# A two-layer decoder trunk on one core: last down tile in two accumulators, down stages in plain order, deferred transposes moved

## The chip, the cores and the metric

One NeuronCore of one Trainium2 chip runs the whole kernel as one program. The metric is device time in microseconds, from the program's start to its end, taken as the median of several executions. Separately, one execution was recorded by the hardware profiler; its trace gives the start and the duration of each instruction on TensorE (PE; its weight loads are PEld), VectorE (DVE), ScalarE (ACT), GpSimd (POOL) and SyncE (SP).

## What is computed

The reference is a two-layer decoder trunk on 256 tokens of width 1024. Cut to what matters here:

```python
def swiglu(x, w_gate, w_up, w_down):
    return (jax.nn.silu(x @ w_gate) * (x @ w_up)) @ w_down

for layer in range(DEPTH):                       # 2 layers
    if layer == N_A_LAYERS:                      # before layer 1
        shared_kv = shared_moba_kv(h, positions, kv_norm_g, w_kv, k_norm_g)
    h = h + 0.5 * swiglu(rms_norm(h, ffn1_norm_g[layer]), ...)
    hn = rms_norm(h, mix_norm_g[layer])
    ...                                          # layer 0: convolution module; layer 1: causal attention
    mem_out = memory_attention(...)              # both layers
    h = h + jnp.concatenate([primary, mem_out], axis=-1) @ w_o[layer]
    h = h + 0.5 * swiglu(rms_norm(h, ffn2_norm_g[layer]), ...)
return h
```

There are four feed-forward blocks of this kind, with an inner width of 2816. All is in 32-bit floating point.

## The kernel before

The four feed-forward blocks are called a, b, c and d and are calls of one function, `ffn` (L353). Everything is kept transposed: features on the 128 partitions, the 256 tokens along the free dimension. A tile of the stream is 128 features, so the width is 8 tiles (`KD`) and the inner width 22 (`KF`).

Precision is bought by splitting. Each weight half-chunk of 128x1024 that the SP queue brings in as `raw` is split into a high part `wh` (a copy on ScalarE that rounds) and a low part `wl` (a subtraction on VectorE). The activations are kept as high and low halves side by side. One product of a 128x128 weight tile with a tile of activations is then high x high, high x low and low x high. There are two ways to issue it:

- `mm2` (L259), a *pair*: one matmul of 512 columns with the high weights over both halves of the activations, and one of 256 columns with the low weights. The result lies in two halves of a PSUM bank, which `both_halves` (L280) adds later: a copy of the second half on ScalarE and an addition on VectorE. `mm2_lo_first` (L271) is the same pair with the low matmul first.
- `mm3` (L252), a *triple*: three matmuls of 256 columns into one half of a bank. It needs no addition afterwards.

Each block has a gate stage and a down stage. In the gate stage, for each of the 22 inner tiles `j`, eight pairs make the gate product (tiles named `ag`, `bg`, `cg`, `dg`) and eight the up product (`au`, `bu`, `cu`, `du`); ScalarE and VectorE turn them into two halves of a hidden tile `hs[:, j]`. In the down stage (L453 to L483), for each of the 8 output tiles `m`, 22 products with the hidden tiles accumulate in one bank (`ao`, `bo`, `co`, `do`). For `m` from 0 to 6 these are pairs, and odd ones have the low matmul first, so the order on TensorE is high, low, low, high, high, low and so on. The last tile, `m` = 7, is 22 triples, so that its eviction is short: the next stage, or the end of the kernel, waits for it. VectorE scales the sum by 0.5 and the norm's factor (`scalar_tensor_tensor`) and adds it to the residual `x` (`tensor_tensor`). Block d then stores each tile.

Small steps are put between the pairs of the gate stage by a plan: a dictionary from (tile `j`, `"g"` or `"u"`, product `k`) to a step. `mean` makes the norm's mean squares (tiny matmuls, `anrp`, `bnrp`, `dnrp`), `rows` spreads the norm's factors over partitions with two transposes (`anbp`, `bnbp`, `cnbp`, `dnbp`). Other planned steps are *turns*: two transposes each that bring a group of keys from token order into head order (`to_heads_T`, L511; tiles `mk1p` for the memory keys of layer 1 in block b, `sk2p` for the last shared keys in block c). In `mm2` a planned step is placed between the pair's high and its low matmul: the transposes are ordered behind the high one, the low one behind the last transpose.

The tile framework schedules each engine's instructions and may change their order, unless the kernel says otherwise. `state["order"]` names engines whose instructions stay in the program's order ("P" is TensorE). Before the change it is "P" from the end of layer 0's output projection (L1139) through block b's first four inner tiles, and empty for the rest of b and for blocks c and d. Layer 1's mixing part between c and d has a list written out by hand (`MIX1`) with all engines in order. The weights flow through three buffers of `raw` and four each of `wh` and `wl`; the accumulators through four PSUM banks, with two more named "aux" for transposes and the like.

Of the kernel before, what the change touches and what calls it, by code (L numbers as in the profile page):

```python
# [9 lines left out]
F32 = mybir.dt.float32  # L10
# [4 lines left out]
ALU = mybir.AluOpType  # L15
AX = mybir.AxisListType

P = 128
# [6 lines left out]
HD = 64  # L25
# [50 lines left out]
e5.a e6.x lo18 e6.h hi19 e7.x e6.l e6.q e7.h lo19 e6.a e7.q e7.a e7.l  # L76
""".split()
AHEAD = 3

POOL_NORM = (1,)  # L80

# [28 lines left out]
def tile_kernel(ctx: ExitStack, tc: tile.TileContext, w, xT, memT, pos, vec, hg, const, spec, out):  # L110
# [39 lines left out]
    nc.vector.memset(mhalf, -0.5)  # L150


    state = {"chunk": 0, "half": 0, "raw": None, "order": "", "last": {}, "between": None, "made": []}

    class Ordered:

# [19 lines left out]
    def behind(i, other):  # L176
        tc.add_manual_dep(i.ins, other.ins.name,
                          mybir.DependencyInfo(mybir.DependencyClass.NoSync, mybir.DependencyReason.DATA),
                          reason="issue order")
# [13 lines left out]
    def mmul(*a, **k):  # L193
        return in_order("P", nc.tensor.matmul(*a, **k))  # L194
# [64 lines left out]
    def mm2(o, wt, y, k, first, last, turn=None):  # L259

        h, l = wt
        a = mmul(o, h, y[:, k].rearrange("p a s -> p (a s)"), start=first, stop=False)
        if turn is not None:
            state["between"] = a
            turn()
            last_turn, state["between"] = state["between"], None
        b = mmul(o[:, :SEQ], l, y[:, k, 0], start=False, stop=last)
        if turn is not None:
            behind(b, last_turn)

    def mm2_lo_first(o, wt, y, k, last):  # L271
        h, l = wt
        mmul(o[:, :SEQ], l, y[:, k, 0], start=False, stop=False)
        mmul(o, h, y[:, k].rearrange("p a s -> p (a s)"), start=False, stop=last)

    def mm_group2(o, y, turns):
        for k, wt in enumerate(tiles_of(1)):
# [51 lines left out]
    def rstd_cols(name, acc):  # L329
        v = mean_cols(name, acc)  # L330
        r = tp.tile([P, NT], F32, name=name, tag="rc", bufs=3)
        gps.tensor_tensor(r, v, mhalf[:, :NT], op=ALU.pow)
        return r
# [17 lines left out]
        return tp.tile([P, SEQ], F32, name=name, tag="acc")  # L351

    def ffn(name, y, acc, nexts, store=False, quick=False, hook=None, after=None, hook_down=None, r=None, plan=None,  # L353
            early=None, turns=()):


        plan = plan or {}
# [9 lines left out]

        def rows():
            norm["rb"] = bcast_rows(name + "nb", norm["r"])
            for turn in turns:  # L370
                turn()

        def planned(j, which):
            return {k: {"mean": mean, "rows": rows}.get(what, what) for (jj, w_, k), what in plan.items()
# [12 lines left out]
        for j in range(KF):  # L387
# [27 lines left out]
            else:  # L415
# [10 lines left out]
                else:  # L426
                    mm_group2(pg, y, planned(j, "g"))
                    mm_group2(pu, y, planned(j, "u"))
            if early and j == 3:
                state["order"] = ""  # L430
            if j == 0 and "mean" not in plan.values() and r is None:
                mean()
            if rb is None and j < rows_at[0]:
# [19 lines left out]
        for m in range(KD):  # L453
            po = psum(f"{name}o{m}")
            if hook_down:
                with tc.issue_after(state["act"].ins):
                    hook_down(m)

            both_sums = m < KD - 1
            for k in range(KF):  # L460
                if both_sums and k % 2:
                    mm2_lo_first(po, next(it), hs, k, k == KF - 1)
                elif both_sums:
                    mm2(po, next(it), hs, k, k == 0, False)
                else:
                    mm3(po[:, :SEQ], next(it), hs, k, k == 0, k == KF - 1)
            if both_sums:
                d = both_halves(f"{name}d{m}", po, "g")
                dve.scalar_tensor_tensor(d, d, 0.5, rb, op0=ALU.mult, op1=ALU.mult)
            else:  # L470
                d = tp.tile([P, SEQ], F32, name=f"{name}d{m}", tag="g")
                dve.scalar_tensor_tensor(d, po[:, :SEQ], 0.5, rb, op0=ALU.mult, op1=ALU.mult)
            dve.tensor_tensor(x[:, m], d, x[:, m], op=ALU.add)
            if store:
                nc.sync.dma_start(out[m], x[:, m])
                continue
            last = quick and m == KD - 1
            if last:
                square_sum(f"{name}q{m}", acc, x[:, m], False, dve)
            for yy, g in zip(ys, nexts):  # L480
                state["ends"] = scaled_split(yy, x[:, m], m, g, last)
            if not last:
                square_sum(f"{name}q{m}", acc, x[:, m], m == 0)  # L483
# [280 lines left out]
    def memory1(m):  # L764
        if not my1:
# [1 line left out]
        mem_prep(1, my1[0], (m,))  # L767

    (y,), acc = ffn("a", y, None, (V_MIX,), quick=True, hook=prepare, after=AF.Exp, hook_down=memory1,
                    plan={(2, "u", 1): "mean", (3, "g", 3): "rows"})  # L770

    hc = cp.tile([P, KF * 2 * SEQ], F32, name="hc", tag="hs")
    taken = [0]
# [368 lines left out]
    def sum_squares():  # L1142
# [7 lines left out]
        for t, tt in found:  # L1150
            key1.normed(t, tt)
        state["order"] = "P"

    (ykv, y), acc = ffn("b", y, acc, (V_KV, V_FFN1 + KD), plan={(2, "u", 1): "mean", (3, "g", 3): "rows"},
                        early=sum_squares, turns=mem_turns)


    rkv = rstd_cols("rkv", acc)
    turns = []
    kuse = [keys(f"sk{i}", rkv, G_K, kTs, 2 * i, True, turns if i == 2 else None, 1) for i in range(3)]  # L1160
# [2 lines left out]
    proj("kv1", ykv, kuse[2], vuse[0])  # L1163
    proj("kv2", ykv, vuse[1], vuse[2])
    (y,), acc = ffn("c", y, acc, (V_MIX + KD,), after=AF.Exp, r=rkv,
                    plan={(2, "g", 4): lambda: [turn() for turn in turns]})
    qT = cp.tile([P, KD, SEQ], F32, name="q1T", tag="t8k")
    cat = y_tiles("cat1")
    ys = y_tiles("oby")
# [307 lines left out]
        steps[name]()  # L1477
    state["order"] = ""
    y, acc = ys, sums
    ffn("d", y, acc, (), store=True, plan={(2, "g", 4): "rows"})  # L1480
    assert state["chunk"] * CH * P == w.shape[0] * CH * P, state


# [147 lines left out]
```

## Time and profile before

| what | value |
|---|---|
| median of 3 executions | 961.93 us (961.75 to 964.14) |
| the profiled execution | 963.06 us |
| its span in the trace | 961.3 us |
| TensorE busy | 953.0 us, 5670 matmuls and as many weight loads |
| VectorE, ScalarE, GpSimd busy | 721.9, 575.1, 90.0 us |

A row of a group tells the line, the engine, the operation, what is written and read (`bo<-bhs,wh`: tile `bo` from the hidden tiles and the high weights), the shape and the number, then durations. L194 and L197 are the helpers through which all matmuls and all transposes are issued, and L164 the one for VectorE, ScalarE and GpSimd, so one goes by the tiles' names. A matmul's recorded duration reaches into the next one, since they are pipelined: what a matmul costs is the distance from its start to the next one's start. A timeline row gives a start and a length in us.

### The profile page before, as it was taken

The page shows a single profiled execution, that of the slowest core. Times are in us where ns is not written, and L with a number is a line of the kernel's source. Part 1 is how long each engine was busy: PE and PEld are TensorE (multiplying, and loading weights), DVE is VectorE, ACT ScalarE, POOL GpSimd, SP SyncE. Part 2 cuts the span into 40 slices and gives each one's busy share as a digit, 9 for nine tenths or more (in the row PEclk, how much of TensorE's full clock was granted, in tenths as well). Part 3 has the DMA queues.
Part 4 walks back from the last instruction along what each step waited for, and adds up shares of the span by engine and source line. Part 5 has one row for each costly group of instructions (what it writes and reads, how often), then busy time and mean ns, then how long its engine had stood idle before and what let it go on. Part 6 is the DMA issues. An engine that isn't in the chain of part 4 may idle for free.

```text
span 961.3 us, 15012 instructions
## 1 busy us (share of the span) xinstructions
PE 953.0 (99%) x5670; PEld 832.1 (87%) x5670; DVE 721.9 (75%) x1263; ACT 575.1 (60%) x1057; POOL 90.0 (9%) x89
## 2 busy tenths in 40 slices
PE   8999999999999999999999999999999999999998
PEld 6888888897888888888988888888897998888887
DVE  6898777776889877767767777767779578777663
ACT  6676566556686655655556665555548666556442
POOL 0122000110012000000123000000134120000000
PEclk9999999999999999999999999999999999999999
DMA  8755455454346555555555555555552245555550
GB/s 293 289 200 188 176 194 200 176 176 152 111 137 222 187 200 175 193 201 176 185 196 189 176 184 208 179 181 205 183 177 74 103 175 182 207 181 182 208 203 21
DMA packets 26569, 174.11 MB, mean 181 GB/s; under 512 B 3329, under 2 KB 4865, under 8 KB 6145
## 3 DMA queue, kind: packets, MB, share of 16 engines
q1 hardware_dynamic: 26208, 172.99, 50.5%
q8 instruction: 44, 0.72, 0.3%
q10 hardware_dynamic: 288, 0.17, 0.1%
q14 instruction: 29, 0.23, 0.1%
HBM read 172.10 MB, written 1.05 MB: 180 GB/s over the span
## 4 chain that ended last, share of the span: by engine, by line
PE 93%; DVE 4%; DMA 1%; ACT 1%; issue 0%; POOL 0%; SPq 0%
PE cg L194 8%; PE do L194 6%; PE ao L194 6%; PE co L194 6%; PE bo L194 6%; PE bu L194 6%; PE dg L194 6%; PE cu L194 6%; PE du L194 6%; PE bg L194 6%; PE ag L194 6%; PE au L194 6%; PE kv L194 3%; PE obo L194 2%; PE mkv L194 2%; DVE room L164 2%
## 5 line engine op out<-in xcount | busy, mean ns | idle before, releaser
L164 DVE TENSOR_TENSOR wl<-raw,wh 128x1024 fp32r<-128x1024 f32 (+1 forms) x326 | 395.8, 1216 | 168.7 <-ACT wh L164 166.8
L164 ACT ACTIVATE wh<-raw 128x1024 fp32r<-128x1024 f32 (+1 forms) x326 | 341.1, 1050 | 296.1 <-PE dg L194 27.1
L194 PE MATMUL ag<-y,wh 128*128 128x512 f32 x176 | 63.7, 398 | 0.5 <-ACT wh L164 0.5
L194 PE MATMUL au<-y,wh 128*128 128x512 f32 x176 | 63.4, 396 | 0.0
L194 PE MATMUL bg<-oay,wh 128*128 128x512 f32 x176 | 62.4, 393 | 0.1
L194 PE MATMUL dg<-oby,wh 128*128 128x512 f32 x176 | 62.5, 392 | 0.0
L194 PE MATMUL cu<-by,wh 128*128 128x512 f32 x176 | 62.3, 393 | 0.0
L194 PE MATMUL du<-oby,wh 128*128 128x512 f32 x176 | 62.3, 391 | 0.0
L194 PE MATMUL cg<-by,wh 128*128 128x512 f32 x176 | 62.2, 392 | 0.0
L194 PE MATMUL bu<-oay,wh 128*128 128x512 f32 x176 | 62.2, 392 | 0.0
L194 PE MATMUL bo<-bhs,wh 128*128 128x512 f32 (+1 forms) x198 | 55.8, 368 | 0.0
L194 PE MATMUL co<-chs,wh 128*128 128x512 f32 (+1 forms) x198 | 55.8, 368 | 0.0
L194 PE MATMUL do<-dhs,wh 128*128 128x512 f32 (+1 forms) x198 | 55.8, 368 | 0.0
L194 PE MATMUL ao<-ahs,wh 128*128 128x512 f32 (+1 forms) x198 | 55.8, 368 | 0.0
L194 PE MATMUL ag<-y,wl 128*128 128x256 f32 x176 | 48.9, 280 | 2.2 <-DVE wl L164 2.2
L194 PE MATMUL cg<-by,wl 128*128 128x256 f32 x176 | 49.4, 281 | 0.0
L194 PE MATMUL bg<-oay,wl 128*128 128x256 f32 x176 | 49.4, 281 | 0.0
L194 PE MATMUL bu<-oay,wl 128*128 128x256 f32 x176 | 49.4, 281 | 0.0
L194 PE MATMUL dg<-oby,wl 128*128 128x256 f32 x176 | 49.4, 280 | 0.0
L194 PE MATMUL cu<-by,wl 128*128 128x256 f32 x176 | 49.3, 280 | 0.0
L194 PE MATMUL du<-oby,wl 128*128 128x256 f32 x176 | 49.3, 280 | 0.0
L194 PE MATMUL au<-y,wl 128*128 128x256 f32 x176 | 48.7, 279 | 0.0
(960 smaller groups left out, 2242.9 us busy)
## 6 DMA issues: line engine op xcount, KB each, us to landing
raw<-in_w SPq DMA_DIRECT2D x158, 1024.0 KB, 4.8
raw<-in_w SPq DMA_DIRECT2D x5, 512.0 KB, 10.4
mT<-in_memT SPq DMA_DIRECT2D x1, 1024.0 KB, 8.4
out<-x SPq DMA_DIRECT2D x8, 128.0 KB, 1.7
dft<-in_spec SPq DMA_DIRECT2D x1, 817.0 KB, 10.2
raw<-in_w SPq DMA_DIRECT2D x2, 256.0 KB, 3.9
x<-in_xT SPq DMA_DIRECT2D x1, 512.0 KB, 8.8
x<-in_xT SPq DMA_DIRECT2D x2, 128.0 KB, 3.2
```

What stands on the lines that cost most here:

```text
L164: i = f(*a, **k)
L194: return in_order("P", nc.tensor.matmul(*a, **k))
```

## The change

Four edits, all in how TensorE's instructions are issued.

1. A planned step is placed behind the pair's low matmul, and the next pair's high matmul is ordered behind it, where it was between the high and the low one.
2. The turns are planned one by one. In b, the two turns of the memory keys, which followed the rows' two transposes directly (six in one place), come one pair and two pairs later. In c, the two turns, planned together at inner tile 2, product 4, are at tile 2, product 6 and at tile 3, product 4.
3. In the down stages of b, c and d all pairs are in plain order (high, low); block a keeps the alternating order. TensorE's program order is kept from inner tile 3 on to the end of these blocks. In the first down tile, behind the third pair, something is computed that nothing reads: in b one bfloat16 matmul of 64 columns, in c two transposes of the identity, in d one product of 256 columns from the pair's own operands.
4. The last down tile of all four blocks is split over two banks: the first 14 products (`APART`) are pairs in one bank, which is evicted and added to `x` while the last 8, as triples, accumulate in another, which is then scaled and added to `x` as before.

```diff
+APART = 14
...
     def mm2(o, wt, y, k, first, last, turn=None):
         h, l = wt
         a = mmul(o, h, y[:, k].rearrange("p a s -> p (a s)"), start=first, stop=False)
-        if turn is not None:
-            state["between"] = a
-            turn()
-            last_turn, state["between"] = state["between"], None
+        if state["held"] is not None:
+            behind(a, state["held"])
+            state["held"] = None
         b = mmul(o[:, :SEQ], l, y[:, k, 0], start=False, stop=last)
         if turn is not None:
-            behind(b, last_turn)
+            state["between"] = b
+            turn()
+            state["held"], state["between"] = state["between"], None
...
+    def unread_little(wt, y):
+        mmul(psum("ul", "aux", 2)[:, :HD], busy[:, :P], busy[:, :HD], start=True, stop=True)
+
+    def unread_product(wt, y):
+        mmul(psum("ue", "aux", 2)[:, :SEQ], wt, y, start=True, stop=True)
+
+    def unread_turns(wt, y):
+        pu = psum("ut", "aux", 2)
+        for i in range(2):
+            transp(pu[:, i * P:(i + 1) * P], ident, ident)
...
-            if early and j == 3:
-                state["order"] = ""
+            if j == 2 and not first:
+                state["order"] = "P"
...
-            both_sums = m < KD - 1
-            for k in range(KF):
-                if both_sums and k % 2:
-                    mm2_lo_first(po, next(it), hs, k, k == KF - 1)
-                elif both_sums:
-                    mm2(po, next(it), hs, k, k == 0, False)
-                else:
-                    mm3(po[:, :SEQ], next(it), hs, k, k == 0, k == KF - 1)
...
+            whole = KF if m < KD - 1 else APART
+            for k in range(whole):
+                if lo_first and k % 2:
+                    mm2_lo_first(po, next(it), hs, k, k == whole - 1)
                 else:
+                    wt = next(it)
+                    mm2(po, wt, hs, k, k == 0, k == whole - 1 and not lo_first,
+                        (lambda: settle(wt[0], hs[:, k, 0])) if settle and (m, k) == (0, 2) else None)
+            d = both_halves(f"{name}d{m}", po, "g")
+            into_x(d, d)
+            if m == KD - 1:
+                po = psum(f"{name}o{m}e")
+                for k in range(APART, KF):
+                    mm3(po[:, :SEQ], next(it), hs, k, k == APART, k == KF - 1)
+                into_x(po[:, :SEQ], tp.tile([P, SEQ], F32, name=f"{name}d{m}e", tag="g"))
...
-                    plan={(2, "u", 1): "mean", (3, "g", 3): "rows"})
+                    plan={(2, "u", 1): "mean", (3, "g", 3): "rows"}, lo_first=True)
...
-    (ykv, y), acc = ffn("b", y, acc, (V_KV, V_FFN1 + KD), plan={(2, "u", 1): "mean", (3, "g", 3): "rows"},
-                        early=sum_squares, turns=mem_turns)
+    (ykv, y), acc = ffn("b", y, acc, (V_KV, V_FFN1 + KD), plan={(2, "u", 1): "mean", (3, "g", 3): "rows", (3, "g", 4): lambda: mem_turns[0](),
+                              (3, "g", 5): lambda: mem_turns[1]()},
+                        early=sum_squares, settle=unread_little)
+    state["order"] = ""
...
-                    plan={(2, "g", 4): lambda: [turn() for turn in turns]})
+                    plan={(2, "g", 6): turns[0], (3, "g", 4): turns[1]}, settle=unread_turns)
...
-    ffn("d", y, acc, (), store=True, plan={(2, "g", 4): "rows"})
+    ffn("d", y, acc, (), store=True, plan={(2, "g", 4): "rows"},
+        settle=unread_product)
```

More of the change, by code (lines that the diff above doesn't have):

```diff
@@ L150, in tile_kernel @@
     nc.vector.memset(mhalf, -0.5)
-    state = {"chunk": 0, "half": 0, "raw": None, "order": "", "last": {}, "between": None, "made": []}
+    state = {"chunk": 0, "half": 0, "raw": None, "order": "", "last": {}, "between": None, "held": None, "made": []}
     class Ordered:
@@ L353, in ffn @@
     def ffn(name, y, acc, nexts, store=False, quick=False, hook=None, after=None, hook_down=None, r=None, plan=None,
-            early=None, turns=()):
+            early=None, settle=None, lo_first=False):
         plan = plan or {}
@@ L369, in rows @@
             norm["rb"] = bcast_rows(name + "nb", norm["r"])
-            for turn in turns:
-                turn()
         def planned(j, which):
@@ L457, in ffn, with into_x @@
                     hook_down(m)
-            both_sums = m < KD - 1
-            for k in range(KF):
-                if both_sums and k % 2:
-                    mm2_lo_first(po, next(it), hs, k, k == KF - 1)
-                elif both_sums:
-                    mm2(po, next(it), hs, k, k == 0, False)
-                else:
-                    mm3(po[:, :SEQ], next(it), hs, k, k == 0, k == KF - 1)
-            if both_sums:
-                d = both_halves(f"{name}d{m}", po, "g")
-                dve.scalar_tensor_tensor(d, d, 0.5, rb, op0=ALU.mult, op1=ALU.mult)
-            else:
-                d = tp.tile([P, SEQ], F32, name=f"{name}d{m}", tag="g")
-                dve.scalar_tensor_tensor(d, po[:, :SEQ], 0.5, rb, op0=ALU.mult, op1=ALU.mult)
-            dve.tensor_tensor(x[:, m], d, x[:, m], op=ALU.add)
+            def into_x(half, d):
+                dve.scalar_tensor_tensor(d, half, 0.5, rb, op0=ALU.mult, op1=ALU.mult)
+                dve.tensor_tensor(x[:, m], d, x[:, m], op=ALU.add)
+            whole = KF if m < KD - 1 else APART
+            for k in range(whole):
+                if lo_first and k % 2:
+                    mm2_lo_first(po, next(it), hs, k, k == whole - 1)
+                else:
+                    wt = next(it)
[8 more added lines that the diff above has]
+                into_x(po[:, :SEQ], tp.tile([P, SEQ], F32, name=f"{name}d{m}e", tag="g"))
             if store:
```

## The prediction

> **What bounds the kernel now.** I read the page first, then TensorE's groups tile by tile, then the timeline of TensorE around every place where something is put between two matmuls. The page has one bottleneck:
>
> ```profile
> span 961.3 us, 15012 instructions
> PE 953.0 (99%) x5670; PEld 832.1 (87%) x5670; DVE 721.9 (75%) x1263; ACT 575.1 (60%) x1057; POOL 90.0 (9%) x89
> PEclk9999999999999999999999999999999999999999
> PE 93%; DVE 4%; DMA 1%; ACT 1%; issue 0%; POOL 0%; SPq 0%
> ```
>
> TensorE is busy 953.0 of 961.3 us at the full granted clock and carries 93% of the chain that ended last. So the time is a sum of start-to-start distances on TensorE, and nothing that other engines gain counts. What is to be seen next is that one pair (a high matmul of 512 columns, a low one of 256) does not always cost the same:
>
> ```profile
> L194 PE MATMUL bg<-oay,wh x145: 391/391/391, 317.2 to 417.1; 128*128 128x512 f32 x145
> L194 PE MATMUL bu<-oay,wh x152: 391/391/391, 317.6 to 419.8; 128*128 128x512 f32 x152
> 319.64 0.39 PE L194 MATMUL bu<-oay,wh 128*128 128x512 f32 x1
> 320.68 0.39 PE L194 MATMUL bg<-oay,wh 128*128 128x512 f32 x1
> L194 PE MATMUL bg<-oay,wh x16: 395/398/403, 302.3 to 310.5; 128*128 128x512 f32 x16
> 304.11 0.40 PE L194 MATMUL bg<-oay,wh 128*128 128x512 f32 x1
> 305.17 0.40 PE L194 MATMUL bu<-oay,wh 128*128 128x512 f32 x1
> ```
>
> The two rows of starts in each half are three pairs apart. In most of block b's gate stage three pairs take 1.04 us (347 ns a pair; the 297 starts of the first two rows, 317.2 to 419.8, give 102.6 / 296 = 346.6). Early in the same stage, with the same instructions and buffers, three pairs take 1.06 us (353.3). I call these the short and the long pace. Durations tell them apart: a high matmul is recorded at 391 in the one and 395 to 403 in the other. Each holds for a long time and turns only where the stream is disturbed. The down stage has a third pace, and its last tile a fourth:
>
> ```profile
> L194 PE MATMUL bo<-bhs,wh x155: 281/392/400, 420.2 to 473.9; 128*128 128x512 f32 x154, 128*128 128x256 f32 x1
> 474.11 0.28 PE L194 MATMUL bo<-bhs,wl 128*128 128x256 f32 x1
> 481.58 0.28 PE L194 MATMUL bo<-bhs,wl 128*128 128x256 f32 x1
> ```
>
> The first row's 155th start opens the last tile, so 154 pairs in alternating order take 53.7 us, 348.7 ns each. The other two are the first and the last low matmul of the last tile: 21 triples in 7.47 us, 355.7 ns each.
>
> **The change part by part.** The last tile: 14 of its 22 triples become pairs. In b, c and d, at the short pace, 14 x (355.7 - 346.7) = 0.13 us each; in a, which keeps the alternating order, 14 x (355.7 - 348.7) = 0.10. Together 0.48 us less. By the Trainium skill (TensorE: Matmul & The Clock Gate, section Back-to-back issue gap) a warm matmul takes 518 cycles of 2.4 GHz for 512 columns and 262 for 256, so a pair would be 780 and a triple 786, 2.5 ns apart, and this edit worth 0.14 us in all instead. The trace disagrees: its triple is 9 ns longer than its pair, and I keep that.
>
> The new eviction adds one copy on ScalarE and three instructions on VectorE, hidden if there is room during the eight triples left (8 x 0.356 = 2.8 us):
>
> ```profile
> L164 ACT ACTIVATE bd6c<-bo 128x256 f32<-128x256 f32 x1 | 0.4, 367 | 0.0
> L164 DVE TENSOR_TENSOR wl<-raw,wh 128x1024 fp32r<-128x1024 f32 x4 | 4.9, 1226 | 2.4 <-ACT wh L164 2.4
> L164 DVE SCALAR_TENSOR_TENSOR bd<-bd,bnb 128x256 f32<-128x256 f32 x1 | 0.4, 424 | 0.0
> ```
>
> 0.37 + 3 x 0.42 = 1.6 us beside one low split of 1.23 us just fits; VectorE waited 2.4 us for ScalarE before such splits between 471 and 482 us. Were it late, the last two VectorE steps of the tile, on which the next stage waits, would slip by some tenths once per block; I count 0, at most 0.3 in all. The end of the kernel keeps the same two steps and the store.
>
> The order in b, c and d's other seven tiles: at the short pace 154 x (348.7 - 346.7) = 0.31 us less each, 0.93 together; at the long pace 154 x (353.3 - 348.7) = 0.71 more each. TensorE's program order, now kept to the end of these stages, brings no wait for the last hidden block:
>
> ```profile
> 425.41 0.42 DVE L164 TENSOR_TENSOR bhs<-bh,bhs 128x256 fp32r<-128x256 f32 x1
> ```
>
> It is there at 425.83. The first tile's 22nd pair, which reads it, would start at 420.2 + 21 x 0.347 = 427.5, 1.7 us later. No transfer is added or moved, and the unread work goes to an auxiliary bank whose last transposes (532.03 in c, below) lie 100 us back, so it waits for nothing but its place.
>
> What is put between pairs, and what the stream does after it:
>
> ```profile
> 518.53 0.28 PE L194 MATMUL cg<-by,wl 128*128 128x256 f32 x1
> 518.65 0.38 PE L197 MATMUL cnbp<-cst,rkv 128*128 128x128 f32 x2
> 518.78 0.48 PE L194 MATMUL cu<-by,wh 128*128 128x512 f32 x1
> 519.10 0.28 PE L194 MATMUL cu<-by,wl 128*128 128x256 f32 x1
> L194 PE MATMUL cu<-by,wh x16: 395/398/476, 518.8 to 527.0; 128*128 128x512 f32 x16
> 528.99 0.38 PE L197 MATMUL sk2p<-cst,sk2t 128*128 128x128 f32 x2
> 529.13 0.48 PE L194 MATMUL cu<-by,wh 128*128 128x512 f32 x1
> L194 PE MATMUL cu<-by,wh x8: 395/398/477, 529.1 to 531.7; 128*128 128x512 f32 x8
> 532.03 0.38 PE L197 MATMUL sk2p<-cst,sk2t 128*128 128x128 f32 x2
> 532.16 0.36 PE L194 MATMUL cg<-by,wl 128*128 128x256 f32 x1
> L194 PE MATMUL cg<-by,wh x155: 390/391/397, 532.4 to 635.7; 128*128 128x512 f32 x155
> ```
>
> These are two transposes three times, each with what follows. Three other cases:
>
> ```profile
> 94.49 0.28 PE L194 MATMUL cbm<-vt,onem 128*128 128x6 f32 x2
> 94.62 0.47 PE L194 MATMUL ag<-y,wh 128*128 128x512 f32 x1
> L194 PE MATMUL ag<-y,wh x72: 392/395/475, 94.6 to 141.5; 128*128 128x512 f32 x72
> 311.17 0.40 PE L194 MATMUL bu<-oay,wh 128*128 128x512 f32 x1
> 311.41 0.50 PE L194 MATMUL bnrp<-onec,oaacc 128*128 128x1 f32 x4
> 311.97 0.39 PE L194 MATMUL bu<-oay,wh 128*128 128x512 f32 x1
> 786.39 0.38 PE L197 MATMUL dnbp<-cst,dnr 128*128 128x128 f32 x2
> 786.53 0.36 PE L194 MATMUL dg<-oby,wl 128*128 128x256 f32 x1
> L194 PE MATMUL dg<-oby,wh x152: 391/391/391, 790.5 to 892.8; 128*128 128x512 f32 x152
> ```
>
> Price first. From 518.53 to 519.10 is one low matmul to the next with two transposes between, 0.57 us where 0.35 is usual: 0.22 for two, and that is c's unread work. The four one-column matmuls at 311.41 stretch one pair from 0.35 to 0.80, 0.11 each. That is my price for b's unread bf16 matmul of 64 columns; its floor is 0, since no row has a lone bf16 matmul in this stream. d's unread product of 256 columns is a third of a triple, 0.12. Together 0.45 more, 0.34 with b's at its floor. The split turns cost what they did, six or four transposes in all, but the last pair of c now comes in the fourth block's gate product, about eight pairs after 532.03, and b's two pairs later: ten pairs longer at the long pace, 0.06.
>
> Sum: -0.48 - 0.93 + 0.45 + 0.06 = -0.90 us. The profiled execution took 963.06 us (961.3 the span, 1.8 around it), so 962.2 for such a one; it lay 1.1 above the median of 961.93, from which the sum gives 961.0.
>
> **Which pace follows.** This decides more than the sum does. In the code before, a planned turn lies between a high matmul and its low one; after, it lies behind the low one and a high one comes next. The rows above hold both. Transposes with a low one next (532.03, 786.39): the short pace follows. Transposes with a high one next (518.65, 528.99): the long pace follows. But both of the latter fell into a stream that was at the long pace already; into a stream at the short pace fell 786.39, and 94.49, which has a high matmul next, and behind both it stayed short (behind 94.49 the 72 gate starts have nine groups, with eight of the up product between them, so 135 steps from 94.6 to 141.5: 347.4 ns, the stretched first one included). So d's turn, which comes into a short stream, and the unread work in the down stages should leave the pace short; b, with three insertions one pair apart, and c, with two places, start from the long one and are open. I take short for all as the likeliest, since every gate stage here ended short.
>
> **The rivals.** First, slower: the turns behind a low matmul leave the gate stage of a block at the long pace to its end. By the rows above, 297 pairs follow the last turn in b, about 2 x 155 in c and 2 x 152 in d; at 6.7 ns that is 2.0, 2.1 and 2.0 us. One block gives 963.0, two 965.1, three 967.1; it decides the sign from the first block on and passes the bound of 0.3% with the second. For it: 518.65 and 528.99. Against it: 94.49, and that b and c have more than one insertion each, so more than one chance to turn.
>
> Second: the gates keep the short pace but the plain order in the down stages falls to the long one, because the unread work turns it or the new tile does. 3 x (0.31 + 0.71) = 3.1 more than forecast, 964.1. In the same group stands the rule of the skill quoted above, by which no order of the same matmuls matters: no gain from the order, 0.48 for the last tile as the rows have it, 0.51 for what is added, so 962.0. Against both: gate and down stages are the same pairs in the same shapes, and 300 of them in a row hold 346.6.
>
> Third, faster: a pace below 346.6. The 911 gate pairs just counted and the 504 down pairs of b, c and d (3 x (7 x 22 + 14)) make 1.4 us of each ns, so from 1.5 ns on it would be 958.9 and less. No stretch of the trace shows one.
>
> **How the numbers follow.** 0.3% of 961.93 is 2.9 us, about what a measurement of this kernel can tell from no change, so "the same" reaches from 959.0 to 964.8. All short: 0.50, 961.0. One block's gates long: 0.13, 963.0. Two or three: 0.21, 965.1 to 967.1. Down stages long, or the order of no account: 0.10, 964.1 or 962.0. Faster pace: 0.06. That is faster 0.06, the same 0.73, slower 0.21. The range 959.9 to 965.6 takes in the first, second and fourth case, the half of the third in which two blocks are long, and the bounds of the unread work and of the runs of before (961.75 to 964.14); the case of three and the faster pace are left out. The first case's own range is 960.3 to 961.8.
>
> **What would show it.** In b, c and d the down tiles' high matmuls of 512 columns number 168, recorded at 391 throughout if short, 395 to 403 if long; tile to tile 7.63 us instead of 7.67; the last tile 7.70 instead of 7.83. Behind each planned turn the first row of the gate tiles tells the pace: 391, or 398. The forecast is wrong if a gate tile of b, c or d shows 398 behind its last turn, if the unread work costs over 0.5 us, or if TensorE shows idle time before the last tile's successor.

## The result, and the profile after

The changed kernel took 967.66 us (median of 5 executions, 966.73 to 968.8) beside 961.93 for the kernel before (5 executions, 961.6 to 964.14): a ratio of 1.0051, with a 95% interval of 1.0034 to 1.0067. It is slower by 0.5%, on the other side of the forecast and outside its range. The profiled execution of after took 967.66 us.

The head of the page of after, and the chain's shares by engine:

```profile
span 965.9 us, 14956 instructions
PE 958.6 (99%) x5618; PEld 831.9 (86%) x5618; DVE 728.1 (75%) x1275; ACT 577.1 (60%) x1061; POOL 89.0 (9%) x89
PEclk9999999999999999999999999999999999999999
PE 93%; DVE 4%; DMA 1%; ACT 1%; POOL 0%; issue 0%; SPq 0%; POOLq 0%
```

TensorE issues 52 matmuls fewer and is busy 5.6 us longer, at the full granted clock, and the chain has its old shares. So no wait was added: the same matmuls stand further apart. The groups by tile (min/median/max of a recorded duration in ns, then the first and the last start) say where:

```profile
L195 PE MATMUL bg<-oay,wh x144: 395/398/403, 319.7 to 418.3; 128*128 128x512 f32 x144
L195 PE MATMUL cg<-by,wh x144: 395/398/403, 540.6 to 639.2; 128*128 128x512 f32 x144
L195 PE MATMUL dg<-oby,wh x152: 391/391/391, 794.9 to 897.2; 128*128 128x512 f32 x152
L195 PE MATMUL bo<-bhs,wh x168: 387/396/475, 421.4 to 480.2; 128*128 128x512 f32 x168
L195 PE MATMUL do<-dhs,wh x168: 387/396/398, 900.3 to 959.0; 128*128 128x512 f32 x168
```

The gate stages of b and c ran at the long pace to their end (395/398/403, where before had 391); d's stayed short. The down stages show something else again: 387/396/398 is neither the 391 of the short pace nor the 395/398/403 of the long one. Two rows of d's down stage, from TensorE's timeline, are 161 pairs apart:

```profile
902.51 0.40 PE L195 MATMUL do<-dhs,wh 128*128 128x512 f32 x1
959.05 0.39 PE L195 MATMUL do<-dhs,wh 128*128 128x512 f32 x1
```

56.54 / 161 = 351.2 ns a pair, where the alternating order before had 348.7 and the short pace would have been 346.7. From the starts in both traces, a gate stage reaching to the first down matmul, a down stage to the first matmul of what follows (for d, where nothing follows, to its last start and 0.12 us more for that matmul):

| stage | before, us | after, us | difference |
|---|---|---|---|
| gate a | 139.10 | 138.67 | -0.43 |
| gate b | 123.82 | 125.80 | +1.98 |
| gate c | 123.06 | 125.38 | +2.32 |
| gate d | 127.17 | 127.17 | 0 |
| down a | 61.53 | 61.42 | -0.11 |
| down b, c, d | 61.52 each | 61.94, 62.05, 61.94 | +0.42, +0.53, +0.42 |

The sum is +5.13, and the span grew by 4.6; the rest of the program was 0.5 shorter. So two questions stand: why b and c kept the long pace, and why a plain down stage doesn't run like a gate stage.

### The profile page after: what moved, and what is told of

It reads as the page before. It is cut to its first block, busy times and chain, and to the rows that moved or that the text cites. A ratio compares the mean times of both kernels' runs of the same rounds, so it can differ in the third digit from the quotient of the medians.

```text
span 965.9 us, 14956 instructions
## 1 busy us (share of the span) xinstructions
PE 958.6 (99%) x5618; PEld 831.9 (86%) x5618; DVE 728.1 (75%) x1275; ACT 577.1 (60%) x1061; POOL 89.0 (9%) x89
## 4 chain that ended last, share of the span: by engine, by line
PE 93%; DVE 4%; DMA 1%; ACT 1%; POOL 0%; issue 0%; SPq 0%; POOLq 0%
PE cg L195 8%; PE bu L195 6%; PE cu L195 6%; PE dg L195 6%; PE du L195 6%; PE bg L195 6%; PE bo L195 6%; PE co L195 6%; PE do L195 6%; PE ag L195 6%; PE au L195 6%; PE ao L195 6%; PE kv L195 3%; PE obo L195 2%; PE mkv L195 2%; DVE room L165 2%
## 5 line engine op out<-in xcount | busy, mean ns | idle before, releaser
L195 PE MATMUL co<-chs,wh 128*128 128x512 f32 x168 | 59.2, 394 | 0.0
L195 PE MATMUL bo<-bhs,wh 128*128 128x512 f32 x168 | 59.1, 394 | 0.0
L195 PE MATMUL do<-dhs,wh 128*128 128x512 f32 x168 | 59.1, 393 | 0.0
L195 PE MATMUL ao<-ahs,wh 128*128 128x512 f32 x168 | 52.5, 393 | 0.0
```

## The experiments

Each kernel is compared with the kernel before on the same chip; the ratio has its 95% interval. "Inside" is the place between a pair's high and its low matmul, "behind" the one behind the low matmul.

The theory after the result had two parts. *Place*: transposes that stand behind a low matmul leave the pace as it is, while those inside may turn it, so that b and c, whose streams are long when the turns come, lost what made them short. *Unread work*: it turns the down stages away from the short pace. Its rival was *own pace*: plain pairs in a down stage run at 351 by themselves.

**Turns inside again (e1).** The change with its planned steps put back inside; all else stays.

```diff
+        if inside is not None:
+            state["between"] = a
+            inside()
+            last_turn, state["between"] = state["between"], None
         b = mmul(o[:, :SEQ], l, y[:, k, 0], start=False, stop=last)
+        if inside is not None:
+            behind(b, last_turn)
...
-            mm2(o, wt, y, k, k == 0, k == KD - 1, turns.get(k))
+            mm2(o, wt, y, k, k == 0, k == KD - 1, None, turns.get(k))
```

> The changed kernel, with the planned steps of the gate stages put back between a pair's high and its low matmul; the turns stay split in twos at their new places, the unread work stays behind a low matmul. Theory 'place' (transposes with a low matmul next bring the short pace, with a high one next they leave the pace that was there): the high matmuls of b's and c's gate stages read 391 behind their last turn instead of 395 to 403, 2.0 us less in each, so about 963.6 us. Rival 'split' (it is the splitting in twos and the later places that keep the long pace): both gate stages stay at 398, 967.7 us.

Measured: 964.73 us (961.92 to 966.89, 10 executions) beside 962.06; ratio 1.0022 (1.0009 to 1.0034). Three lie at 961.9 to 962.4, three at 963.7 to 964.9, four at 965.6 to 966.9. The profiled one was the fastest; its gate rows:

```profile
L195 PE MATMUL bg<-oay,wh x145: 391/391/392, 314.9 to 414.8; 128*128 128x512 f32 x145
L195 PE MATMUL cg<-by,wh x145: 391/391/392, 533.8 to 633.6; 128*128 128x512 f32 x145
```

Both blocks are short, and nothing else differs from after, whose fastest execution (966.73) is slower than nine of these ten. So the place does decide over these two stages, but not in one way for all executions: 2 us is the price of one gate stage at the long pace, and a spread of 5 us would fit none, one or two long ones. The times alone don't show how many, since block a's gate stage by itself took 137.1 to 139.3 us in the traces. Nor is the place all of it. The median still lies 2.7 us above the kernel before. The down stages cost 1.3 of that in this trace; 1.4 are left for gate stages in which the turns are still split in twos. What the split costs wasn't separated.

**No unread work (e2, e3).** In the change (e2) and in e1 (e3), `settle` is `None` in b, c and d.

```diff
-                        early=sum_squares, settle=unread_little)
+                        early=sum_squares, settle=None)
...
-                    plan={(2, "g", 6): turns[0], (3, "g", 4): turns[1]}, settle=unread_turns)
+                    plan={(2, "g", 6): turns[0], (3, "g", 4): turns[1]}, settle=None)
...
-        settle=unread_product)
+        settle=None)
```

> The changed kernel without the three pieces of unread work; nothing else. Theory 'unread' (the unread work itself brings the down stages to 351 ns a pair): d's down stage, whose first three pairs took 346 ns, stays there, 0.8 us less beside 0.12 for the work; b and c, whose first pairs took 352, keep about that, 0.33 less; together about 966.4 us. Rival 'own pace' (351 ns is what plain order takes in a down stage): d's down pairs go to 351 by themselves, and only 0.45 us goes, 967.2 us.

> Both edits together: planned steps between the high and the low matmul, no unread work. By 'place' and 'unread' all gate stages and all three plain down stages run at 346 to 347 ns a pair: 4.0 + 0.45 + 3 x 0.8 less than the changed kernel, 960.8 us, below the kernel before. By 'place' and 'own pace' 963.2 us, with down stages at 351.

Measured, e2: 966.04 us (965.8 to 967.23, 4 executions), ratio 1.0038 (1.0024 to 1.0052). Its b and c gates are long again. d's down stage, which follows a short gate stage and has nothing put into it:

```profile
L195 PE MATMUL do<-dhs,wh x168: 386/396/400, 898.7 to 957.3; 128*128 128x512 f32 x168
```

58.6 us from the first to the last start, as in after (58.7) less the unread product's 0.12, and the same mixed durations. "Unread work" falls: 351 ns is the plain down stage's own pace here. The three stages took 61.83, 61.83 and 61.81 us, so the unread work cost 0.11, 0.22 and 0.13.

e3: 964.55 us (961.68 to 966.79, 10 executions), ratio 1.0019 (1.0007 to 1.0031), spread like e1. Its profiled execution (965.98 us) had b short and c long, and shows in c both things that an insertion inside can do. TensorE's timeline at c's two turns, and the tile's row behind them:

```profile
529.98 0.38 PE L198 MATMUL sk2p<-cst,sk2t 128*128 128x128 f32 x2
530.11 0.36 PE L195 MATMUL cg<-by,wl 128*128 128x256 f32 x1
...
534.83 0.40 PE L195 MATMUL cg<-by,wh 128*128 128x512 f32 x1
535.06 0.38 PE L198 MATMUL sk2p<-cst,sk2t 128*128 128x128 f32 x2
535.20 0.36 PE L195 MATMUL cg<-by,wl 128*128 128x256 f32 x1
```

```profile
L195 PE MATMUL cg<-by,wh x145: 395/398/403, 536.1 to 637.9; 128*128 128x512 f32 x145
```

By the starts in the trace, three pairs took 1.06 us before the first turn and 1.04 after it; behind the second they take 1.06 again, and the last row shows that pace to the end of the stage. Inside isn't "turns it short"; it is a new draw.

**The last tile alone (e4).** The kernel before with its last down tile in two banks, 14 alternating pairs and 8 triples; nothing else.

```diff
...
+            whole = KF if m < KD - 1 else APART
+            for k in range(whole):
+                if k % 2:
+                    mm2_lo_first(po, next(it), hs, k, k == whole - 1)
...
+            if m == KD - 1:
+                po = psum(f"{name}o{m}e")
+                for k in range(APART, KF):
+                    mm3(po[:, :SEQ], next(it), hs, k, k == APART, k == KF - 1)
...
```

> The kernel before with the split of the last down tile alone (14 pairs in alternating order, then 8 triples in a second bank). Both theories of the pace: no pace changes, four last tiles at 14 x 7.0 ns less, 0.4 us in all, 961.5 us. Rival (the added eviction makes VectorE late for the last two steps): up to 0.3 us more per block, 962.3 or above.

Measured: 961.67 us (960.53 to 963.04, 11 executions) beside 962.06; ratio 0.9993 (0.9985 to 1.0002). All four down stages took 61.41 to 61.42 us in the trace, 0.11 less than the 61.53 of before, so 0.44 in all, as the medians say (0.39). The time alone doesn't tell it from no change; the trace does.

**Behind alone (e5).** The kernel before with the new `mm2` only: the planned steps behind the low matmul, all where the old plan has them: six transposes together in b, and in c the two turns, which the trace shows apart (527.88 and 530.80).

```diff
+        if state["held"] is not None:
+            behind(a, state["held"])
+            state["held"] = None
         b = mmul(o[:, :SEQ], l, y[:, k, 0], start=False, stop=last)
         if turn is not None:
-            behind(b, last_turn)
+            state["between"] = b
+            turn()
+            state["held"], state["between"] = state["between"], None
```

> The kernel before with one edit of the change alone: planned steps behind the low matmul. The turns stay where they were and together, the down stages stay in alternating order with triples in the last tile. Theory 'keeps' (work put behind a low matmul keeps the pace it finds, work put between high and low draws it anew and mostly gets the short one): b and c come with the long pace to their only planned transposes and keep it, gate high matmuls 398 to the end, 2.0 and 2.1 us more, about 966.0 us. Rival 'split' (twos at later places are what leaves it long): both turn to 391, 962.0 us.

Measured: 965.16 us (961.68 to 966.97, 10 executions) beside 961.69; ratio 1.0025 (1.0012 to 1.0038), spread like e1. The profiled execution was again the fastest one, with every gate stage short, and its timeline is a counterexample to a strict "behind keeps":

```profile
314.28 0.38 PE L197 MATMUL bnbp<-cst,bnr 128*128 128x128 f32 x2
314.50 0.60 PE L197 MATMUL mk1p<-cst,mk1t 128*128 128x128 f32 x4
314.85 0.47 PE L194 MATMUL bg<-oay,wh 128*128 128x512 f32 x1
```

The stream was long up to 314.28; behind these six transposes it was short. So the move alone costs time in most executions (six of the ten took 965.05 us or more), and place is a matter of odds. Whether six transposes together turn a stream more easily than the twos of after, one trace can't tell.

**One inside per block (e6), and its variants (e7, e8).** From e3: b's rows and c's first turn inside, b's turns, c's second turn and d's rows behind. e7 moves the hidden tiles against the weights by two pads that nothing reads, 128 bytes a partition ahead of the hidden tiles and 1920 behind them. The hidden tiles move by 128 bytes, and the weights and the streams of the gate stages, whose buffers lie behind them, by 2048; counted modulo 4096, hidden tiles and streams then stand alike to the weights. e8 is e6 with every down stage alternating.

```diff
e6, against e3:
-            mm2(o, wt, y, k, k == 0, k == KD - 1, None, turns.get(k))
+            step = turns.get(k)
+            if isinstance(step, Behind):
+                mm2(o, wt, y, k, k == 0, k == KD - 1, step.step)
+            else:
+                mm2(o, wt, y, k, k == 0, k == KD - 1, None, step)
...
e7, against e6:
+        if acc is None:
+            pad = cp.tile([P, 32], F32, name="pad0")
+            nc.gpsimd.memset(pad, 0.0)
         hs = cp.tile([P, KF, 2, SEQ], F32R, name=name + "hs", tag="hs")
+        if acc is None:
+            pad = cp.tile([P, 480], F32, name="pad1")
+            nc.gpsimd.memset(pad, 0.0)
e8, against e6:
-                if lo_first and k % 2:
+                if k % 2:
...
```

> The changed kernel without unread work, in which one planned step of each block that comes at the long pace is put between high and low (b's rows, c's first turn) and every later one behind a low matmul (b's two turns, c's second, d's rows). Theory 'keeps': the first brings the short pace and the later ones keep it, so b, c and d read 391 to the end of their gate stages in nearly every execution, where three or two steps between high and low gave 961.7 to 966.9 us over ten executions; here 961.4 to 962.2 us, the down stages still at 351. Rival 'chance' (any step draws anew): executions spread over 961.5 to 966 us as before.

> The kernel e6_one_inside with the hidden tiles' buffer moved by 128 bytes against the weights (two unread tiles of 128 and 1920 bytes before and behind it), so that moving operand and weights stand in the down stages as they do in the gate stages, modulo 4096 bytes; nothing else. Theory 'address' (the operands' relative place makes a down pair 351 ns in plain order): down high matmuls at 391 throughout, 168 x 4.5 ns less in each of b, c and d, 2.3 us less than e6_one_inside, about 959.5 us. Rival 'stage' (22 products in one bank, or what else a down stage has): 351 ns as before, the same time as e6_one_inside.

> The kernel e6_one_inside with all four down stages in alternating order again; the last tile stays split in pairs and triples. It would be the best by 'keeps' and 'stage': three down stages at 348.6 in place of 351.1 ns, 1.2 us less than e6_one_inside, and below the kernel before by the last tile's 0.4 us and by its executions with a long gate stage: 960.5 to 961.0 us with little spread. Rival: the pace of the gate stages is drawn anew all the same, 961 to 965 us.

Measured beside 961.69: e6 964.53 us (963.91 to 965.84, 8 executions), ratio 1.0024 (1.0014 to 1.0034); e7 963.34 (960.09, then 962.7 to 963.78, 10 executions), ratio 1.0009 (0.9999 to 1.0018); e8 963.21 (961.11 to 965.27, 12 executions), ratio 1.0015 (1.0005 to 1.0025). Gates and a down stage of e6:

```profile
L195 PE MATMUL bg<-oay,wh x144: 395/398/403, 319.2 to 417.8; 128*128 128x512 f32 x144
L195 PE MATMUL cg<-by,wh x145: 391/391/391, 536.8 to 636.6; 128*128 128x512 f32 x145
L195 PE MATMUL co<-chs,wh x155: 387/396/400, 639.8 to 693.8; 128*128 128x512 f32 x155
```

c is short, but not by its turns: its rows, two transposes at 522.12 that the plan doesn't place, had a low matmul next and turned it before them, and neither the turn inside nor the one behind changed that. b is long (125.81 us for the stage, 123.8 where it is short) although its rows were inside. The executions of e6 lie within 2 us of each other, where those of e1 and e5 spread over 5, which fits a b that is long each time. And c's down stage follows a gate stage at 346.7 and still runs at 351. Now the down stages of e7:

```profile
L195 PE MATMUL bo<-bhs,wh x150: 395/398/403, 421.1 to 473.8; 128*128 128x512 f32 x150
L195 PE MATMUL co<-chs,wh x154: 391/391/391, 640.3 to 693.3; 128*128 128x512 f32 x154
```

The shift changed the down stage's pace: 391 throughout in c, and in d too, 61.11 us for c's stage where e6 had 61.81. And b's runs at the long pace of the gate stage ahead of it (62.24 us). With the hidden tiles moved, a plain down stage simply takes over its gate stage's pace. Without the move it ran at 351 behind a short gate stage (d) and behind a long one (b and c of after), so it is the address, and not what lies ahead, that gives this pace. That the place relative to the weights counts is argued: in the gate stages, which kept their paces, stream and weights moved together. Which of the two shifts does it wasn't separated. In e8 the alternating stages of b, c and d took 61.39 to 61.40 us, where e4 has 61.41: at the old addresses the alternating order is the better one. e8's executions still spread over 4 us; its trace has b's gate stage long and c's and d's short.

**b's turns: apart (e9), together inside (e10).** e9 is e7 with block a plain too and b's two turns behind a pair of inner tiles 4 and 5, in place of one and two pairs after the rows. e10 is e9 with b's turns directly behind the rows inside (six transposes), as the kernel before has them.

```diff
e9, against e7:
-(3, "g", 4): Behind(lambda: mem_turns[0]()),
-                              (3, "g", 5): Behind(lambda: mem_turns[1]())},
+(4, "g", 4): Behind(lambda: mem_turns[0]()),
+                              (5, "g", 4): Behind(lambda: mem_turns[1]())},
...
-                    plan={(2, "u", 1): "mean", (3, "g", 3): "rows"}, lo_first=True)
+                    plan={(2, "u", 1): "mean", (3, "g", 3): "rows"})
e10, against e9:
             norm["rb"] = bcast_rows(name + "nb", norm["r"])
+            for turn in turns:
+                turn()
...
```

> The kernel e7_hidden_moved with block a's down stage in plain order too, and b's two turns behind low matmuls at inner tiles 4 and 5 instead of one and two pairs behind the rows. Theory 'keeps when settled' (work behind a low matmul keeps the pace if the stream has settled, and b was long in e6 to e8 because its turns came one pair after the rows): b, c and d short in nearly every execution, all four down stages at 346.7, 959.6 to 960.1 us, below the kernel before. Rival 'chance in b' (b's rows themselves draw the long pace there, wherever the turns are): b long in most executions and its down stage with it, about 963 us.

> The kernel e9_turns_apart with b's rows and two turns in one place between a high and a low matmul, as in the kernel before. By 'keeps when settled': short in b in most executions, as in the kernel before, 959.6 to 960.1 us with a few at 962.5. By 'chance in b': the same time as e9_turns_apart, both spread.

Measured beside 961.93: e9 961.38 us (960.73 to 963.85, 11 executions, nine of them under 961.8), ratio 0.9997 (0.9988 to 1.0006); e10 960.87 (960.1 to 962.25, 11 executions), ratio 0.9988 (0.9979 to 0.9997). Both have b, c and d short, gates (in e9 with the two turnings shown next) and down stages (61.11 us). In e9, b's stream changed its pace twice more behind the rows; the timeline, and the tile's row behind it:

```profile
319.41 0.47 PE L195 MATMUL bg<-oay,wh 128*128 128x512 f32 x1 [0.28 <-DVE bgs L165]
...
321.24 0.38 PE L198 MATMUL mk1p<-cst,mk1t 128*128 128x128 f32 x2
```

```profile
L195 PE MATMUL bg<-oay,wh x130: 391/391/396, 327.7 to 416.8; 128*128 128x512 f32 x130
```

A wait of 0.28 us for VectorE at 319.41 turned short to long, the first turn behind kept it long, the second, at 327.11, turned it short. So a wait can change the pace as an insertion can.

Both runs lie above the 959.6 to 960.1 us expected of them, 0.95 us of it in block a's plain down stage: it took 62.06 us, 352 ns a pair, where 61.11 was counted on, though its hidden tiles are the moved ones too. That mean hides two paces. TensorE's program order isn't kept in block a, and in e9's trace two high and then two low matmuls stand together at one place. The rows of the stage ahead of it, the place, and the rows behind it:

```profile
L195 PE MATMUL ao<-ahs,wh x25: 392/392/395, 143.2 to 151.5; 128*128 128x512 f32 x25
...
151.82 0.62 PE L195 MATMUL ao<-ahs,wh 128*128 128x512 f32 x2
152.28 0.40 PE L195 MATMUL ao<-ahs,wl 128*128 128x256 f32 x2
...
L195 PE MATMUL ao<-ahs,wh x140: 395/398/403, 152.9 to 202.0; 128*128 128x512 f32 x140
```

The first 25 pairs took 346.6 ns each, the pace of a's gate stage ahead of them; those behind the place took 353.4, to the end. e10 has the same at 152.17. So the moved buffer holds the short pace in block a too, until a change of order turns the stream.

**The change itself with the buffer moved (e11).** After, with e7's two pads.

> The changed kernel as it is, unread work and all, with the hidden tiles' buffer moved by 128 bytes against the weights. By 'address' and 'keeps' the down stages take over the pace of their gate stages: d at 346.7 instead of 351.1 (0.74 us less), b and c, whose gates are long, at 353.3 (0.37 more each), the same total as the changed kernel, 967.6 us. If the unread work draws the pace anew, b's or c's down stages come to 346.7 behind it, 0.7 to 1.5 us less.

Measured: 964.03 us (963.4 to 966.4, 10 executions) beside 961.93; ratio 1.0023 (1.0014 to 1.0033), where the change without the move has 1.0051. The profiled execution was the slowest of the ten; eight took 963.4 to 964.3 us, and what they did otherwise isn't known. Its b and c gates were long; the unread matmul of b, then the rows of both down tiles:

```profile
422.21 0.20 PE L195 MATMUL ul<-busy 128*128 128x64 bf16 x1
```

```profile
L195 PE MATMUL bo<-bhs,wh x152: 391/391/475, 422.2 to 474.7; 128*128 128x512 f32 x152
L195 PE MATMUL co<-chs,wh x154: 395/398/476, 641.4 to 695.7; 128*128 128x512 f32 x154
```

Where the pairs can hold the short pace, the one unread bfloat16 matmul turned b's down stage from long to short (61.26 us, with the unread work in it), while c's two transposes kept the long one (62.45) and d's product the short one (61.23). At the old address every plain down stage of b, c and d in these traces ran at 351, whatever was put into it.

**All together (e12).** e10 with block a alternating again: six transposes inside in b, c with one turn inside and one behind, d's rows behind, plain down stages on the moved buffer in b, c and d, the last tile in two banks, no unread work.

```diff
-                    plan={(2, "u", 1): "mean", (3, "g", 3): "rows"})
+                    plan={(2, "u", 1): "mean", (3, "g", 3): "rows"}, lo_first=True)
```

> The kernel e10_turns_together with block a's down stage in alternating order, since e10's ran at 352 ns a pair in plain order and e7's at 349 in alternating order. By 'address' and the pace table: b, c and d as in e10, a's down stage 61.42 instead of 62.06 us, so 0.6 us less than e10_turns_together: 960.2 us, 1.7 below the kernel before. Rival: a's pace in plain order was drawn and not the order's, then no gain, 960.9 us.

Measured: 959.88 us (959.36 to 962.11, 11 executions) beside 961.43 (15 executions); ratio 0.9985 (0.9976 to 0.9994). It beats both kernels, by 1.55 us against before. A gate tile and a down tile:

```profile
L195 PE MATMUL bg<-oay,wh x145: 391/391/391, 314.9 to 414.7; 128*128 128x512 f32 x145
L195 PE MATMUL bo<-bhs,wh x155: 391/391/391, 417.9 to 471.2; 128*128 128x512 f32 x155
```

This is what the prediction had expected of the change: 391 from the first pair behind the rows to the last one of the down stage.

**The fourteen traces together.** Two to six transposes stand between gate matmuls in many places. Counted here are those with three undisturbed pairs ahead of them and, beyond the first, two or more behind. Inside (a low matmul next): all 31 that came into a long stream were followed by a short one; of 38 that came into a short stream 32 left it short and 6 turned it long. Behind (a high one next): 26 of 26 left a short stream short, and 18 of 20 left a long one long. So behind keeps, nearly always; inside turns a long stream short, and mostly leaves a short one so.

Five of the six that turned long have something in common. The short pace comes in two forms. In the even one each pair takes 346 or 347 ns, and every high matmul reads 391; in the alternating one pairs of 350 and 343 ns follow each other, and the high ones read 395 and 392. Of the 33 insertions inside that came into the even form 32 left the stream short; all five that came into the alternating form turned it long. But these five are one place, the rows of block c, in five traces (after, e2, e3, e7, e11), so that the form decides is not shown for any other.

## Why the prediction was wrong

**Two gate stages at the long pace: +4.3 us. This is the step that failed.** The prediction put it as "I take short for all as the likeliest, since every gate stage here ended short", with b and c "open". They ended short in the kernel before because the last insertion in each had a low matmul next, and the change takes this placement away. Its rows had the answer: both insertions with a high matmul next (518.65, 528.99) left a long stream long, and the one with a low matmul next (532.03) turned it. In after, b's three insertions stand behind low matmuls, and three pairs behind the last one take 1.07 us by these rows (316.49 to 317.56), where 1.04 would be short:

```profile
314.78 0.38 PE L198 MATMUL bnbp<-cst,bnr 128*128 128x128 f32 x2
314.92 0.48 PE L195 MATMUL bg<-oay,wh 128*128 128x512 f32 x1
...
315.93 0.38 PE L198 MATMUL mk1p<-cst,mk1t 128*128 128x128 f32 x2
316.06 0.48 PE L195 MATMUL bg<-oay,wh 128*128 128x512 f32 x1
316.49 0.40 PE L195 MATMUL bg<-oay,wh 128*128 128x512 f32 x1
...
317.56 0.40 PE L195 MATMUL bu<-oay,wh 128*128 128x512 f32 x1
```

c came to the same end in another way. In after its stream was short, in the alternating form, until its rows, which stand at a place that no plan gives and here have a low matmul next:

```profile
520.94 0.39 PE L195 MATMUL cu<-by,wh 128*128 128x512 f32 x1
521.98 0.40 PE L195 MATMUL cu<-by,wh 128*128 128x512 f32 x1
522.56 0.38 PE L198 MATMUL cnbp<-cst,rkv 128*128 128x128 f32 x2
522.69 0.36 PE L195 MATMUL cu<-by,wl 128*128 128x256 f32 x1
523.24 0.40 PE L195 MATMUL cg<-by,wh 128*128 128x512 f32 x1
524.30 0.40 PE L195 MATMUL cg<-by,wh 128*128 128x512 f32 x1
```

Three pairs take 1.04 us ahead of them and 1.06 behind. The two turns (531.38, 536.54), now with high matmuls next, left that as it was, where the one at 532.03 of the kernel before had ended it.

"More than one insertion each, so more than one chance to turn" counted draws where there are hardly any. The first rival had this mechanism, and its price held: 2.0 and 2.1 us a block forecast, 1.98 and 2.32 measured. What e1, e3 and e5 add is that the place doesn't settle it alone: b and c end short in five of their six gate stages traced and long in one, and their executions spread over 5 us. That one program gives both paces is read from these times; each has one trace.

**d's turn: right.** It came into a short stream behind a low matmul and left it short, as forecast and as 26 of 26 do.

**Plain order in b, c and d: -0.93 forecast, +1.1 measured.** The term failed at "gate and down stages are the same pairs in the same shapes, and 300 of them in a row hold 346.6". They are the same in shape and not in address. At this address a plain pair takes 351.2 ns, against 348.7 in the alternating order: 154 x 2.5 = 0.38 more in each stage, where the prediction had 0.31 less. e7 settles it: with the buffers shifted the same pairs take 346.7. The second rival (the long pace, 0.71 each) had the sign and not the size, and its cause, unread work that turns the stage, was wrong. By the Trainium skill (TensorE: Matmul & The Clock Gate, section Back-to-back issue gap) a warm matmul's isolated gap goes by its columns alone, so that a pair would cost the same in any order and at any address; here they have at least four: 346.7, 348.7, 351.2 and 353.3 ns.

**The last tile: right.** -0.48 forecast; e4 has -0.11 per block, 0.44 in all. In after the pairs of b, c and d are the 351.2 ones, so that it was 14 x 4.5 = 0.06 there. The new eviction was free: the last tile's VectorE work of block b starts 0.2 us behind the next stage's first matmul, which waits for nothing.

```profile
483.37 0.39 PE L195 MATMUL kv<-wh,by 128*128 128x512 f32 x1
L165 DVE SCALAR_TENSOR_TENSOR bd7e<-bo7e,bnb x1: 425/425/425, 483.6 to 483.6; 128x256 f32<-128x256 f32 x1
```

**The unread work: right in price.** 0.11, 0.22 and 0.12 forecast, 0.11, 0.22 and 0.13 measured. It did nothing else in after, though e11 shows that in another layout it can turn a stage.

**The sum.** 961.0 forecast, 967.66 measured. The gates of b and c make 4.3 of the 6.7 us between them and the down stages of b, c and d 2.2 (+1.37 instead of -0.87). Block a's gate stage and the rest of the program were 0.9 shorter, and the forecast had taken 1.1 off its profile to come to the median, while the profile of after is the median itself: 4.3 + 2.2 - 0.9 + 1.1 = 6.7.

**Left open.** Why b stays long in e6, e7 and e8 when its rows are inside: the turns behind follow one pair later, before the new pace can be read, and e9, with the turns apart, and e10, with all inside, are short; that the turns came too close is argued and not shown. In e7 the rows also came into the alternating short form, which the five above turned long. What splitting the turns in twos costs by itself. Why executions of one program differ. What in TensorE makes the paces, and why the buffers' place counts. And block a's gate stage, nearly the same instructions in all fourteen traces, took 137.1 to 139.3 us, which is part of any difference between two executions.

## What to carry to other kernels

On a stream of matmuls that is the bound, read the distances between starts before and behind each insertion, and ask of a moved step what the place that it leaves was doing: "every stage ends well" may be the work of the very place that is given up. Equal shapes don't make equal paces: when a loop is to take over another one's pace, compare the operands' addresses as well, and try a shift of the buffer, which here cost 2 KB a partition. Where executions of one program spread, a profile of one shows one draw; take ten times beside it.

## What the runs showed of the hardware

- The same stream of 512- and 256-column matmuls, each with its own weight load, runs at 346.7 or 353.3 ns a pair at a granted clock of 1.00, for hundreds of pairs, until something stands between two matmuls or their order changes. The recorded duration of the high one mostly tells them apart: 395 to 403 in the long pace, 391 in the even form of the short one, 392 and 395 in turn in its alternating form (block a's down stage in e9).
- A pause of 0.28 us (e9), two transposes (e3), one 64-column bfloat16 matmul (e11) or two high matmuls in a row (block a in e9) stood where the pace changed. Executions of one program spread over 5 us (e1, e5).
- Where the buffers lie decides whether these paces are to be had: with the hidden tiles 128 bytes and the weights 2048 bytes further on, a pair of the down stage took 346.7 instead of 351 ns (e7 against e6, blocks c and d).
- In alternating order (high, low, low, high) all sixteen down stages with the last tile in two banks took 61.39 to 61.42 us, behind long and short gate stages and with old and moved buffers alike (e4, e8, and block a of eight other runs): an order that never reaches the best pace here but isn't subject to the draw.
